# Norm sums turned one projection later, two projections issued ahead, and the rotary additions on GpSimd, in a two-layer hybrid encoder

## The chip, the cores and the metric

The kernel runs on one core of a Trainium2 chip. The metric is the device time of one execution in microseconds (us), lower is better; the time before is the median of three runs.

## The reference, cut to what matters

Two layers work on 512 tokens of width 1024. In each, one projection of the normalised input feeds three token mixers, which are gated, merged and projected out; a conv-gated MLP follows.

```python
h = RMSNorm(x); proj = h @ w_in          # one wide projection, split into
#  A: neighbourhood attention, 4 heads of 64, q and k RMS-normed per head
#  B: sliding-window attention, 8 q heads, 2 k/v heads, q/k normed, rotary on both
#  C: gated DeltaNet, 4 heads, chunks of 64 tokens, RMS-normed and gated output
#  merge gates: 3 x 1024 sigmoid gates
def apply_rope(x, cos, sin):
    x1, x2 = xf[..., :half], xf[..., half:]
    return jnp.concatenate([x1 * c - x2 * s, x2 * c + x1 * s], axis=-1)
```

The change touches the per-head norms of A's and B's queries and keys, and the rotation in B.

## The kernel before, in words

**Layout.** Activations lie as features on partitions and tokens along the free axis, in tiles of 128 x 512. A dense product is cut into chunks of 128 output features; `dense(l, c, rs)` makes one chunk. Weights and inputs are split in a high and a low part, and each of a chunk's 8 k-tiles takes three matmuls of 128 x 512 (`mm3`, L152 to L154: high by high, low by high, high by low), so a chunk is 24 matmuls. Its weights come in two halves of 4 k-tiles (256 KB each): SyncE's queue starts the transfer, ScalarE rounds the high part `wh` (L142), VectorE subtracts to get the low part `wl` (L144); for the chunks of the MLP GpSimd does that. Three buffers each hold raw, high and low halves.

**The projections of B** (`swa_project`): one chunk of keys (CH_SK), one of values (CH_SV), four of queries (CH_SQ to CH_SQ+3). **Of A** (`na_project`): twice a chunk of queries, keys and values (CH_NA+3j to CH_NA+3j+2). The first chunk of C's keys is CH_GK.

**A norm** squares the projection on ScalarE (`sq`) and calls `sums`: four small matmuls (L187) add the squares of each head into `pb`; ScalarE copies them to `sb` (L80); a TensorE transposition (L191) puts tokens on partitions. VectorE then computes the inverse root in nine short operations (`rsq`, L173 to L180). `spread` writes the factors into a 128 x 512 tile `rb` on VectorE (L201), four TensorE transpositions (L205) bring them back to the features' layout, and for a key L304 multiplies. Queries keep their factors by token, so only keys (`knorm`) and the output of C (`gdn_out`) use `spread`.

**The rotation** (`rope`, five times a layer: one key and four query tiles): a transfer by SyncE's queue makes `sw` with halves exchanged, GpSimd multiplies by the cosine (L310, `raw<-raw,fix`), VectorE multiplies `sw` by the sine (L311), and VectorE adds both (L312, `raw<-raw,sw`). Then ScalarE, VectorE and GpSimd split the result into `kdh`/`kdl` or `qs` (L476, L477, L504, L505).

**Order.** The stages are written in the order `sp np gg na gp sa gx gz gs gm gc go mn ms mg` (B's projections, A's projections, C's gates, A's attention, C's projections, B's attention, C's recurrence, its output `go`, the merges). Within that a scheduler of the framework picks the order of instructions on each engine when the kernel is built, and buffer pools limit it. `behind(m)` pins what stands in it to come after instruction `m` on its engine; `lastm[0]` is the last dense matmul written so far; `made` holds a chunk that was issued before its place. Dense chunks without a dependency (gates of the merges, for instance) are what the scheduler puts between small dependent steps.

**C's end** (`gdn_out`, twice a layer, j = 0 and 1): 32 small matmuls (L904, L908, tile `gd`), the square (L910), `sums`, L914, `rsq`, `spread`, and the gate (L916). Lines move in the changed kernel: L187 becomes L191, L191 becomes L198, L201 becomes L209, L205 becomes L213, L904 and L908 become L918 and L922, L310 to L312 become L322 to L324, L322 becomes L334, L477 becomes L489, L496 becomes L510.

Of the kernel before, what the change touches and what calls it, by code (L numbers as in the profile page):

```python
# [12 lines left out]
ALU = mybir.AluOpType  # L13
# [48 lines left out]
def encoder_kernel(ctx, tc, xT, wall, par, cst, nab, out, depth=2, dbg=None):  # L62
# [82 lines left out]
            ws += [(hi[:, k], lo[:, k]) for k in range(n)]  # L145
        return ws

    lastm, made = [None], {}

    def mm3(acc, w, r, start, stop):  # L150
        (wh, wl), (rh, rl) = w, r
# [1 line left out]
        T.matmul(acc, lhsT=wh, rhs=rl, start=False, stop=False)  # L153
        lastm[0] = T.matmul(acc, lhsT=wl, rhs=rh, start=False, stop=stop)  # L154

    def dense(l, c, rs):
        if (l, c) in made:
            return made.pop((l, c))
        ws = load_w(l, c)
        acc = bank("mm")  # L160
        for k, r in enumerate(rs):
            mm3(acc, ws[k], r, k == 0, k == len(rs) - 1)
        return acc

    def split(src, hi, lo):
# [16 lines left out]


    def sums(src, sel, tag, pb=None):
        pb = bank(tag)[:, 0:256] if pb is None else pb
        for b in range(4):
            T.matmul(pb[32 * b:32 * b + 32, 0:128], lhsT=sel, rhs=src[:, 128 * b:128 * b + 128], start=True, stop=True,  # L187
                     tile_position=(0, 32 * b))
        sb = tmp(shape=(128, 128), name="sb")
        copy("sb", sb, pb[:, 0:128])  # L190
        T.transpose(pb[:, 128:256], sb, ident)  # L191
        return pb[:, 128:256].rearrange("p (b i) -> p b i", b=4)[:, :, 0:32:16]


    def behind(m):
# [90 lines left out]
    for l in range(depth):  # L286
# [7 lines left out]
        y, mg, ma = {}, [], [None] * 8  # L294


        def knorm(raw, gain, dst, m=None):
            sq = tmp(name="sq")
            S.activation(out=sq, in_=raw, func=AF.Square)
            pb = sums(sq, halves, "at")  # L300
            a = small(8, "ka")
            V.tensor_scalar(a.rearrange("p (b e) -> p b e", e=2), pb, HD * EPS, None, op0=ALU.add)
            pr = spread(rsq(a, 8).rearrange("p (b e) -> p b e", e=2), 8.0, "at", m)
            V.scalar_tensor_tensor(dst, raw, gain, pr, op0=ALU.mult, op1=ALU.mult)  # L304

        def rope(qn):
            sw = tmp(name="sw")
            for b in range(4):
                nc.sync.dma_start(out=sw[32 * b:32 * b + 32], in_=qn[32 * (b ^ 1):32 * (b ^ 1) + 32])
            on("cos", "G").tensor_tensor(qn, qn, cosT, op=ALU.mult)  # L310
            on("sin", "V").tensor_tensor(sw, sw, sinT, op=ALU.mult)  # L311
            on("ropa", "V").tensor_tensor(qn, qn, sw, op=ALU.add)  # L312
            return qn

        def perm(a):
# [41 lines left out]
        def na_project():  # L357
            line[0] = "n"
            nonlocal naqk, vt, vt4, rns, irn

            xa = tmp(name="xa")
            S.activation(out=cr(xa), in_=perm(strm.acc), func=AF.Copy)
            naqk = []
            vt = [tmp(shape=(128, 4, 128), name="nvt") for _ in range(2)]
            vt4 = tmp(shape=(128, 4, 128), name="nvt4")
            pb = sums(xa, one, "at")
            an = small(16, "an")
            anv = an.rearrange("p (b f) -> p b f", f=4)
            mp = small(4, "mp")
            V.tensor_scalar(mp, pb[:, :, 0], HD * EPS / D, HD * EPS * EPS, op0=ALU.mult, op1=ALU.add)  # L370
            for j in range(2):
                qn, kn = tmp(name="qn"), tmp(name="kn")
                vn = tmp(name="nav")
                acc = dense(l, CH_NA + 3 * j, h)
                S.activation(out=cr(qn), in_=perm(acc), func=AF.Copy, scale=P[:, P_QK:P_QK + 1])
                sq = tmp(name="sq")
                S.activation(out=cr(sq), in_=perm(acc), func=AF.Square)
                pb = sums(sq, halves, "at")
                V.tensor_tensor(anv[:, :, 2 * j:2 * j + 2], mp.unsqueeze(2).to_broadcast([128, 4, 2]),
                                pb, op=ALU.add)  # L380
                kraw = permuted(dense(l, CH_NA + 3 * j + 1, h), tmp(name="raw"))
                permuted(dense(l, CH_NA + 3 * j + 2, h), vn)
                if j:
                    made[l, CH_GK] = dense(l, CH_GK, h)
                knorm(kraw, P[:, P_QK + 1:P_QK + 2], kn, lastm[0])
                qp, kh, kl = pair(F32R, name="nqs"), pair(F32R, name="nkh"), pair(F32R, name="nkl")
                naqk.append((qp, kh, kl))
                for e in range(2):
                    r = slice(64 * e, 64 * e + 64)
                    o = slice(64 - 64 * e, 128 - 64 * e)  # L390
                    S.activation(out=qp[e][r], in_=qn[r], func=AF.Copy)
                    on("nql", "G").tensor_tensor(qp[e][o], qn[r], qp[e].bitcast(F32)[r], op=ALU.subtract)
                    copy("nkh", kh[e][r], kn[r], "V")
                    S.activation(out=kh[e][o], in_=kn[r], func=AF.Copy)

                    on("nkl", "V").tensor_tensor(kl[e][r], kn[r], kh[e].bitcast(F32)[r], op=ALU.subtract)
                    G.memset(kl[e].bitcast(F32)[o], 0.0)
                pt = bank("at")
                for b in range(4):
                    k0, kn0 = (0, 64) if b == 0 else (128 * b - 64, 128)  # L400
                    T.transpose(pt[0:kn0, 128 * b:128 * b + 128], vn[:, k0:k0 + kn0], ident)
                S.activation(out=vt[j][0:64, 0], in_=pt[0:64, 0:128], func=AF.Copy)
                S.activation(out=vt[j][:, 1:4], in_=pt[:, 128:512].rearrange("p (b m) -> p b m", b=3), func=AF.Copy)
                pt = bank("at")
                T.transpose(pt[0:64, 0:128], vn[:, 448:512], ident)
                S.activation(out=vt4[0:64, j], in_=pt[0:64, 0:128], func=AF.Copy)
            rn = rsq(an, 16)
            rns = kept("rns", 16)
            V.tensor_scalar(rns, rn, -RSQ, None, op0=ALU.mult)
            irn = kept("irn", 16)  # L410
            V.scalar_tensor_tensor(irn, an, -1.0, rns, op0=ALU.mult, op1=ALU.mult)
# [53 lines left out]
        def swa_project():  # L465
            line[0] = "a"
            nonlocal kdh, kdl, vst, qs, rqs
            kr = scaled(dense(l, CH_SK, h), tmp(name="raw"))
            knorm(kr, P[:, P_QK + 3:P_QK + 4], kr)
            kr = rope(kr)  # L470
            kdh, kdl = pair(F32R, name="kdh"), pair(F32R, name="kdl")
            for gq in range(2):
                r = slice(64 * gq, 64 * gq + 64)
                o = slice(64 - 64 * gq, 128 - 64 * gq)
                copy("kdh", kdh[gq][r], kr[r], "V")
                S.activation(out=kdh[gq][o], in_=kr[r], func=AF.Copy)  # L476
                V.tensor_tensor(kdl[gq][r], kr[r], kdh[gq].bitcast(F32)[r], op=ALU.subtract)  # L477
                G.memset(kdl[gq].bitcast(F32)[o], 0.0)
            vf = scaled(dense(l, CH_SV, h), tmp(name="vf"))
            vst = tmp(name="sv")  # L480
            pt = bank("at")
            for b in range(4):
                T.transpose(pt[:, 128 * b:128 * b + 128], vf[:, 128 * b:128 * b + 128], ident)
            S.activation(out=vst, in_=pt, func=AF.Copy)

            qs = []
            aq = kept("aq")
            aqv = aq.rearrange("p (b f) -> p b f", f=8)
            for j in range(4):  # L489
                acc = dense(l, CH_SQ + j, h)  # L490
                qr = tmp(name="raw")
                S.activation(out=qr, in_=acc, func=AF.Copy, scale=P[:, P_QK + 2:P_QK + 3])
                sq = tmp(name="sq")
                S.activation(out=sq, in_=acc, func=AF.Square)
                pb = sums(sq, halves, "at")
                V.scalar_tensor_tensor(aqv[:, :, 2 * j:2 * j + 2], ms.unsqueeze(2).to_broadcast([128, 4, 2]), HD * EPS / D,  # L496
                                       pb, op0=ALU.mult, op1=ALU.add)
                qr = rope(qr)
                qp = pair(F32R, name="qs")
                for e in range(2):  # L500
                    r = slice(64 * e, 64 * e + 64)
                    o = slice(64 - 64 * e, 128 - 64 * e)
                    t = qp[e]
                    S.activation(out=t[r], in_=qr[r], func=AF.Copy)  # L504
                    on("ql", "G").tensor_tensor(t[o], qr[r], t.bitcast(F32)[r], op=ALU.subtract)  # L505
                qs.append(qp)
            rq = rsq(aq, 32)
            rqs = kept("rqs")
            V.tensor_scalar(rqs, rq, -RSQ, None, op0=ALU.mult)
# [664 lines left out]
```

## Time and profile before

| | |
|---|---|
| median of 3 runs | 1661.05 us (1659.44 to 1661.3) |
| the profiled execution, its own time | 1657.82 us |
| its span on the core | 1656.0 us |
| granted TensorE clock, mean | 0.998 |
| TensorE busy (matmuls) | 1626.6 us |
| VectorE busy | 1009.8 us |
| ScalarE busy | 767.0 us |
| GpSimd busy | 530.1 us |

The span is what the profiler saw from the first to the last instruction; 1.8 us of the execution lie outside it. A busy time is the sum over an engine's instructions. In the rows below PE is TensorE, DVE is VectorE, ACT is ScalarE, POOL is GpSimd; `out<-in` names the tiles with their buffer numbers left out, and an arrow in brackets names who ended a wait.

### The profile page before, as it was taken

How to read it: one execution, taken by the hardware profiler on the slowest of the kernel's cores; microseconds unless marked ns; L12 is line 12 of the kernel's file. 1: busy time of each engine (PE TensorE's matmuls, PEld its weight loads, DVE VectorE, ACT ScalarE, POOL GpSimd, SP SyncE). 2: the span in 40 equal slices, each digit the busy share in tenths (PEclk: the TensorE clock that was granted, in tenths of full speed). 3: DMA queues.
4: the chain of work that ended last, by engine and by line, in shares of the span. 5: the costliest groups of instructions: out<-in, count | busy, mean ns of one | idle time of the engine just before them, and what ended most of it. 6: DMA issues, size and time to landing. Idle time of an engine off the chain costs nothing.

```text
span 1656.0 us, 25095 instructions
## 1 busy us (share of the span) xinstructions
PE 1626.6 (98%) x9196; PEld 1300.2 (79%) x9196; DVE 1009.8 (61%) x1907; ACT 767.0 (46%) x1500; POOL 530.1 (32%) x512
## 2 busy tenths in 40 slices
PE   7999999998999999999999999999999999999999
PEld 5777787676888888878887777876788888888887
DVE  5699895454747777741137998855566577777200
ACT  5556666522444444443335665664234444444321
POOL 0333210130035554554406231102200455455543
PEclk9999999999999999999999999999999999999999
DMA  6222221121532323244333222111225322223442
GB/s 211 87 80 74 86 74 37 33 93 54 184 122 90 99 93 100 95 128 137 125 107 103 80 69 77 52 39 40 89 88 180 115 95 95 99 95 110 134 134 73
DMA packets 91499, 160.45 MB, mean 97 GB/s; under 512 B 10352, under 2 KB 17136, under 8 KB 91376
## 3 DMA queue, kind: packets, MB, share of 16 engines
q1 hardware_dynamic: 91376, 158.85, 29.7%
q8 instruction: 72, 1.18, 0.3%
q14 instruction: 51, 0.42, 0.1%
HBM read 147.80 MB, written 8.39 MB: 94 GB/s over the span
## 4 chain that ended last, share of the span: by engine, by line
PE 85%; DVE 5%; issue 4%; POOL 3%; ACT 2%; DMA 1%; SPq 0%; POOLq 0%; DVEq 0%; ACTq 0%
PE mm L152 24%; PE mm L154 24%; PE mm L153 24%; POOL wl L144 2%; PE at L560 1%; PE at L553 1%; DVE wl L144 1%; PE gd L710 1%; PE at L529 1%; PE at L456 1%; PE gd L843 1%; PE at L530 1%; PE gd L875 1%; PE gd L825 1%; PE gd L346 0%
## 5 line engine op out<-in xcount | busy, mean ns | idle before, releaser
L152 PE MATMUL mm<-hh,wh 128*128 128x512 f32 x1408 | 557.5, 396 | 11.2 <-ACT wh L142 9.9
L154 PE MATMUL mm<-hh,wl 128*128 128x512 f32 x1408 | 555.9, 395 | 5.2 <-DVE wl L144 5.1
L153 PE MATMUL mm<-hl,wh 128*128 128x512 f32 x1408 | 554.9, 395 | 0.5 <-DVE hl L222 0.5
L144 POOL TENSOR_TENSOR wl<-wr,wh 128x512 fp32r<-128x512 f32 (+1 forms) x272 | 363.3, 1347 | 556.7 <-ACT wh L142 545.3
L142 ACT ACTIVATE wh<-wr 128x512 fp32r<-128x512 f32 (+1 forms) x512 | 312.5, 617 | 328.1 <-PE mm L153 222.1
L152 PEld LDWEIGHTS mm<-hh,wh 128*128 128x128 f32 x1408 | 265.9, 189 | 71.5 <-ACT wh L142 12.4
L154 PEld LDWEIGHTS mm<-hh,wl 128*128 128x128 f32 x1408 | 265.9, 189 | 66.0 <-DVE wl L144 9.2
L153 PEld LDWEIGHTS mm<-hl,wh 128*128 128x128 f32 x1408 | 265.8, 189 | 59.0 <-DVE hl L222 3.0
L144 DVE TENSOR_TENSOR wl<-wr,wh 128x512 fp32r<-128x512 f32 x240 | 174.8, 731 | 97.9 <-ACT wh L142 93.5
L245 DVE SCALAR_TENSOR_TENSOR cv<-up,fix,cv 128x511 f32<-128x511 f32 x88 | 143.1, 1626 | 2.8
L154 PE MATMUL mm<-act,wl 128*128 128x512 f32 x352 | 137.1, 390 | 0.6 <-POOL wl L144 0.6
L244 DVE SCALAR_TENSOR_TENSOR cv<-up,fix,cv 128x511 f32<-128x511 f32 x88 | 83.0, 945 | 89.7 <-ACT cv L243 89.7
L152 PE MATMUL mm<-act,wh 128*128 128x512 f32 x352 | 137.1, 389 | 0.3 <-ACT wh L142 0.3
L153 PE MATMUL mm<-act,wh 128*128 128x512 f32 x352 | 137.0, 389 | 0.0
L243 ACT ACTIVATE cv<-up,fix 128x512 f32<-128x512 f32 x88 | 70.8, 809 | 35.5 <-DVE up L291 35.5
L166 ACT ACTIVATE act<-cv 128x512 fp32r<-128x512 f32 x44 | 27.8, 632 | 126.9 <-DVE cv L995 126.9
L154 PEld LDWEIGHTS mm<-act,wl 128*128 128x128 f32 x352 | 66.1, 188 | 15.3 <-POOL wl L144 1.2
L152 PEld LDWEIGHTS mm<-act,wh 128*128 128x128 f32 x352 | 66.1, 188 | 14.2 <-ACT wh L142 0.7
L153 PEld LDWEIGHTS mm<-act,wh 128*128 128x128 f32 x352 | 66.1, 188 | 13.7
L872 POOL TENSOR_TENSOR sd<-SA,fix 64x256 f32<-64x256 f32 x24 | 15.5, 646 | 177.5 <-DVE SA L882 135.5
L1013 DVE TENSOR_TENSOR xo<-xo,mm 128x512 f32<-128x512 f32 x8 | 5.5, 688 | 105.1 <-PE mm L154 105.1
L994 ACT ACTIVATE cv<-cv 128x512 f32<-128x512 f32 x44 | 27.8, 632 | 83.8 <-DVE cv L245 83.8
(292 smaller groups left out, 2153.1 us busy)
## 6 DMA issues: line engine op xcount, KB each, us to landing
wr<-in_wall_dram SPq DMA_DIRECT2D x496, 256.0 KB, 2.8
xs<-xo SPq DMA_DIRECT2D x16, 256.0 KB, 2.2
xo<-xs SPq DMA_DIRECT2D x16, 256.0 KB, 3.9
sw<-raw SPq DMA_DIRECT2D x40, 64.0 KB, 2.0
xf<-in_xT_dram SPq DMA_DIRECT2D x8, 256.0 KB, 6.2
xo<-in_xT_dram SPq DMA_DIRECT2D x8, 256.0 KB, 3.4
xf<-xs SPq DMA_DIRECT2D x8, 256.0 KB, 3.8
wr<-in_wall_dram SPq DMA_DIRECT2D x16, 128.0 KB, 3.1
```

The costliest lines, as they stand in the source:

```text
L142: S.activation(out=hi[:, :n], in_=raw[:, :n], func=AF.Copy)
L144: (G if c >= CH_UP else V).tensor_tensor(lo[:, :n], raw[:, :n], hi.bitcast(F32)[:, :n], op=ALU.subtract)
L152: T.matmul(acc, lhsT=wh, rhs=rh, start=start, stop=False)
L153: T.matmul(acc, lhsT=wh, rhs=rl, start=False, stop=False)
L154: lastm[0] = T.matmul(acc, lhsT=wl, rhs=rh, start=False, stop=stop)
L166: S.activation(out=hi, in_=src, func=AF.Copy)
L243: S.activation(out=dst, in_=src, func=AF.Identity, scale=w[:, 1:2], bias=bias)
L244: V.scalar_tensor_tensor(dst[:, 1:L], src[:, 0:L - 1], w[:, 0:1], dst[:, 1:L], op0=ALU.mult, op1=ALU.add)
L245: V.scalar_tensor_tensor(dst[:, 0:L - 1], src[:, 1:L], w[:, 2:3], dst[:, 0:L - 1], op0=ALU.mult, op1=ALU.add)
L456: T.matmul(py[64 * e:64 * e + 64, 128 * b_:128 * b_ + 128], lhsT=(vt[j][0:wi, b_ + i] if b_ + i < 4 else vt4[0:wi, j])[:, 64 * e:64 * e + 64],
L529: T.matmul(sc[:, 0:w], lhsT=q_, rhs=kdh[gq][:, kc], start=True, stop=False)
L994: S.activation(out=cv[0], in_=cv[0], func=AF.Silu)
```

## The change

The transposition of the norm sums is cut off from `sums` (`sums_from` returns `by_token(m)`), and is pinned behind the dense chunk that follows. For B's queries that chunk is issued ahead (`made`). `knorm` gets `first` (the values' projection, done between its sums and their transposition) and `then` (a chunk that is issued ahead; the transpositions of the factors are pinned behind it). So the value projection of B moves ahead of the key's rotation. And the rotation's addition moves from VectorE to GpSimd. `sums` is now `sums_from` with its transposition at once. The argument `m` of `dense` is not used.

```diff
+    def sums_from(src, sel, tag, pb=None):
         pb = bank(tag)[:, 0:256] if pb is None else pb
         ...
         copy("sb", sb, pb[:, 0:128])
-        T.transpose(pb[:, 128:256], sb, ident)
-        return pb[:, 128:256].rearrange("p (b i) -> p b i", b=4)[:, :, 0:32:16]
+        def by_token(m):
+            with behind(m):
+                lastt[0] = T.transpose(pb[:, 128:256], sb, ident)
+            return pb[:, 128:256].rearrange("p (b i) -> p b i", b=4)[:, :, 0:32:16]
+        return by_token
...
-        def knorm(raw, gain, dst, m=None):
+        def knorm(raw, gain, dst, first, then):
             sq = tmp(name="sq")
             S.activation(out=sq, in_=raw, func=AF.Square)
-            pb = sums(sq, halves, "at")
+            by_token = sums_from(sq, halves, "at")
+            first()
+            pb = by_token(lastm[0])
+            made[l, then] = dense(l, then, h)
+            m = lastm[0]
...
-            on("ropa", "V").tensor_tensor(qn, qn, sw, op=ALU.add)
+            on("ropa", "G").tensor_tensor(qn, qn, sw, op=ALU.add)
...
-                pb = sums(sq, halves, "at")
+                by_token = sums_from(sq, halves, "at")
+                kraw = permuted(dense(l, CH_NA + 3 * j + 1, h), tmp(name="raw"))
+                pb = by_token(lastm[0])
...
-                kraw = permuted(dense(l, CH_NA + 3 * j + 1, h), tmp(name="raw"))
-                permuted(dense(l, CH_NA + 3 * j + 2, h), vn)
-                if j:
-                    made[l, CH_GK] = dense(l, CH_GK, h)
-                knorm(kraw, P[:, P_QK + 1:P_QK + 2], kn, lastm[0])
+                knorm(kraw, P[:, P_QK + 1:P_QK + 2], kn, lambda: permuted(dense(l, CH_NA + 3 * j + 2, h), vn),
+                      CH_GK if j else CH_NA + 3)
...
-            knorm(kr, P[:, P_QK + 3:P_QK + 4], kr)
+            vf = tmp(name="vf")
+            knorm(kr, P[:, P_QK + 3:P_QK + 4], kr, lambda: scaled(dense(l, CH_SV, h), vf), CH_SQ)
...
-            vf = scaled(dense(l, CH_SV, h), tmp(name="vf"))
...
-                pb = sums(sq, halves, "at")
+                by_token = sums_from(sq, halves, "at")
+                nxt = CH_SQ + j + 1 if j < 3 else CH_NA
+                made[l, nxt] = dense(l, nxt, h)
+                pb = by_token(lastm[0])
```

The scheduler places everything else anew. On TensorE the matmuls are the same in both kernels; their order differs only within two stretches, one in each layer, from B's projections to the end of C.

**VectorE, layer 0, behind B's first query projection.** `kdh` and `kdl` are the key's split after its rotation, `nav` is A's value projection scaled, L311 or L323 the sine, L496 or L510 a query's sums. Before:

```order
L496 SCALAR_TENSOR_TENSOR fix<-fix,at 128x4x2
L312 TENSOR_TENSOR raw<-raw,sw 128x512
L496 SCALAR_TENSOR_TENSOR fix<-fix,at 128x4x2
L81 CAST kdh<-raw 64x512
L81 CAST kdh<-raw 64x512
L322 TENSOR_TENSOR nav<-mm,rstd 128x512
L311 TENSOR_TENSOR sw<-sw,fix 128x512
L477 TENSOR_TENSOR kdl<-raw,kdh 64x512
L477 TENSOR_TENSOR kdl<-raw,kdh 64x512
L144 TENSOR_TENSOR wl<-wr,wh 128x512
L312 TENSOR_TENSOR raw<-raw,sw 128x512
```

Of the change:

```order
L510 SCALAR_TENSOR_TENSOR fix<-fix,at 128x4x2
L334 TENSOR_TENSOR nav<-mm,rstd 128x512
L323 TENSOR_TENSOR sw<-sw,fix 128x512
L81 CAST kdh<-raw 64x512
L81 CAST kdh<-raw 64x512
L144 TENSOR_TENSOR wl<-wr,wh 128x512
L489 TENSOR_TENSOR kdl<-raw,kdh 64x512
L489 TENSOR_TENSOR kdl<-raw,kdh 64x512
L144 TENSOR_TENSOR wl<-wr,wh 128x512
```

Both additions are gone, and the weights' `wl` stands ahead of the key's `kdl` instead of behind it.

**TensorE, layer 0, the end of C's first half** (tile `gd_3111` is its sums, `gd_3130` its factors; `mm` are dense chunks of the merge gates). Before, after the last L908 of this half there are 22 dense matmuls, the sums (L187), 21 more dense matmuls, and then:

```order
L153 MATMUL mm_4243<-hl_151,wh_4239 128x512
L191 MATMUL gd_3111<-fix,sb_3116 128x128
L154 MATMUL mm_4243<-hh_150,wl_4241 128x512
L152 MATMUL mm_4243<-hh_159,wh_4239 128x512
L153 MATMUL mm_4243<-hl_160,wh_4239 128x512
L154 MATMUL mm_4243<-hh_159,wl_4241 128x512
L205 MATMUL gd_3130<-fix,rb_3128 128x128 x4
```

Of the change:

```order
L918 MATMUL gd_3074<-qd_474_2138,SA_2898 64x64
L918 MATMUL gd_3074<-qd_475_2139,SA_2898 64x64
L922 MATMUL gd_3074<-Q_2125,VN_2782 64x64 x2
L191 MATMUL gd_3111<-sq_3108,fix 32x128 x4
L198 MATMUL gd_3111<-fix,sb_3116 128x128
L213 MATMUL gd_3130<-fix,rb_3128 128x128 x4
L918 MATMUL gd_3140<-qd_476_2140,SA_2895 64x64
```

No dense matmul is left from the half's last L922 to its factors' transpositions; those chunks now stand ahead, between the steps of C's recurrence. On VectorE nothing stands within that chain (L928 to L209) any more; before, L291 (`gt`) and one L144 did.

**TensorE, layer 1, the same place.** Before, 21 dense matmuls lie between the sums and L191 and 37 between L191 and L205, which ends so:

```order
L154 MATMUL mm_11989<-hh_7447,wl_11981 128x512
L152 MATMUL mm_11989<-hh_7561,wh_11985 128x512
L153 MATMUL mm_11989<-hl_7562,wh_11985 128x512
L205 MATMUL gd_10876<-fix,rb_10874 128x128 x4
L904 MATMUL gd_10886<-qd_2078_9886,SA_10641 64x64
```

Of the change, again with 21 dense matmuls between the sums and the first row's transposition:

```order
L198 MATMUL gd_10857<-fix,sb_10862 128x128
L154 MATMUL mm_11989<-hh_7789,wl_11987 128x512
L152 MATMUL mm_11989<-hh_7903,wh_11985 128x512
L153 MATMUL mm_11989<-hl_7904,wh_11985 128x512
L154 MATMUL mm_11989<-hh_7903,wl_11987 128x512
L213 MATMUL gd_10876<-fix,rb_10874 128x128 x4
L918 MATMUL gd_10886<-qd_2078_9886,SA_10641 64x64
```

Four dense matmuls are left between the two, and in VectorE's row one `gt` and one `wl` still stand within the chain.

## Rows read from the trace of the kernel before

**Rows 1.** The page: busy time of the engines, and the chain that ended last.

```profile
PE 1626.6 (98%) x9196; PEld 1300.2 (79%) x9196; DVE 1009.8 (61%) x1907; ACT 767.0 (46%) x1500; POOL 530.1 (32%) x512
PE 85%; DVE 5%; issue 4%; POOL 3%; ACT 2%; DMA 1%; SPq 0%; POOLq 0%; DVEq 0%; ACTq 0%
```

**Rows 2.** TensorE's waits, 60 to 160 us: us in total, times, longest.

```profile
PE mm L154 <- DVE wl L144: 1.8, 2, 1.3
PE mm L152 <- DVE kn L304: 1.1, 1, 1.1
PE at L205 <- DVE rb L201: 0.8, 1, 0.8
PE at L187 <- DVE abd L586: 0.7, 1, 0.7
```

**Rows 3.** TensorE's waits, 860 to 960 us.

```profile
PE mm L154 <- DVE wl L144: 1.7, 1, 1.7
PE mm L152 <- ACT wh L142: 1.5, 1, 1.5
PE at L191 <- ACT sb L80: 1.1, 1, 1.1
```

**Rows 4.** TensorE's waits, 260 to 430 us: recurrence and end of C, layer 0.

```profile
PE gd L205 <- DVE rb L201: 2.6, 1, 2.6
...
PE gd L875 <- DVE VN L866: 0.6, 1, 0.6
...
PE gd L863 <- DVE SA L880: 0.3, 1, 0.3
```

**Rows 5.** VectorE's row around 75 us: start, duration.

```profile
72.98 0.69 DVE L144 TENSOR_TENSOR wl<-wr,wh 128x512 fp32r<-128x512 f32 x1
...
77.10 1.77 DVE L144 TENSOR_TENSOR wl<-wr,wh 128x512 fp32r<-128x512 f32 x1
```

**Rows 6.** GpSimd's row in the same stretch.

```profile
69.79 1.29 POOL L310 TENSOR_TENSOR raw<-raw,fix 128x512 f32<-128x512 f32 x1 [1.53 <-DMA sw<-raw]
75.08 4.94 POOL L505 TENSOR_TENSOR qs<-raw,qs 64x512 fp32r<-64x512 f32 x3 [4.00 <-ACT qs L504]
```

**Rows 7.** Line L312, the additions: duration in ns (least, median, most), idle before.

```profile
L312 DVE TENSOR_TENSOR raw<-raw,sw x10: 679/692/1780, 66.4 to 903.5; 128x512 f32<-128x512 f32 x10
...
  POOL raw L310: 4.9, 3
```

**Rows 8.** TensorE, end of C's first half, layer 0: start, duration.

```profile
374.40 0.29 PE L908 MATMUL gd<-Q,VN 128*64 128x64 f32 x4
...
379.83 0.46 PE L187 MATMUL gd<-sq,fix 128*32 128x128 f32 x8
...
385.16 0.27 PE L191 MATMUL gd<-fix,sb 128*128 128x128 f32 x1
...
388.95 0.66 PE L205 MATMUL gd<-fix,rb 128*128 128x128 f32 x4 [2.61 <-DVE rb L201]
```

**Rows 9.** ScalarE in the same place.

```profile
374.79 0.60 ACT L910 ACTIVATE sq<-gd 128x512 f32<-128x512 f32 x1 [0.84 <-PE gd L908]
...
380.53 0.26 ACT L80 ACTIVATE sb<-gd 128x128 f32<-128x128 f32 x1
```

**Rows 10.** VectorE in the same place.

```profile
385.46 0.17 DVE L914 TENSOR_TENSOR fix<-gd,fix 128x8 f32<-128x8 f32 x1 [0.74 <-PE gd L191]
...
386.39 0.69 DVE L291 TENSOR_TENSOR gt<-mm,rstd 128x512 f32<-128x512 f32 x1
...
387.07 0.68 DVE L144 TENSOR_TENSOR wl<-wr,wh 128x512 fp32r<-128x512 f32 x1
...
388.47 0.43 DVE L201 TENSOR_SCALAR rb<-fix 128x512 f32<-128x512 f32 x1
```

**Rows 11.** TensorE, the same place in layer 1.

```profile
1200.01 0.27 PE L191 MATMUL gd<-fix,sb 128*128 128x128 f32 x1
...
1208.53 0.60 PE L205 MATMUL gd<-fix,rb 128*128 128x128 f32 x4
```

More of the change, by code (lines that the diff above doesn't have):

```diff
@@ L146, in load_w @@
         return ws
-    lastm, made = [None], {}
+    lastm, lastt, made = [None], [None], {}
     def mm3(acc, w, r, start, stop):
@@ L154, in mm3, with dense @@
         lastm[0] = T.matmul(acc, lhsT=wl, rhs=rh, start=False, stop=stop)
-    def dense(l, c, rs):
+    def dense(l, c, rs, m=None):
         if (l, c) in made:
@@ L160, in dense @@
         acc = bank("mm")
-        for k, r in enumerate(rs):
-            mm3(acc, ws[k], r, k == 0, k == len(rs) - 1)
+        with behind(m):
+            for k, r in enumerate(rs):
+                mm3(acc, ws[k], r, k == 0, k == len(rs) - 1)
         return acc
@@ L184, in sums @@
     def sums(src, sel, tag, pb=None):
+        return sums_from(src, sel, tag, pb)(None)
+    def sums_from(src, sel, tag, pb=None):
         pb = bank(tag)[:, 0:256] if pb is None else pb
@@ L190, in sums @@
         copy("sb", sb, pb[:, 0:128])
-        T.transpose(pb[:, 128:256], sb, ident)
-        return pb[:, 128:256].rearrange("p (b i) -> p b i", b=4)[:, :, 0:32:16]
+        def by_token(m):
+            with behind(m):
+                lastt[0] = T.transpose(pb[:, 128:256], sb, ident)
+            return pb[:, 128:256].rearrange("p (b i) -> p b i", b=4)[:, :, 0:32:16]
+        return by_token
     def behind(m):
```

## The prediction

> **What bounds the kernel now.** I read the page first: TensorE is busy 98% of the span and holds 85% of the chain that ended last [rows 1]. So the time is the sum of TensorE's work and its waits, and the built order has the same matmuls in both kernels; a matmul that only changes its place costs nothing. What can change is where TensorE stands still. The list of its waits over the two stretches in which the order differs says how much there is to win: 4.4 us in four kinds of place in layer 0's projections [rows 2], 4.3 us in layer 1's [rows 3], and in the recurrence and end of C one wait of 2.6 us and small ones of 0.9 us together [rows 4]. The largest gain that this change can make is thus 8.7 us from the projections and 3.5 us behind them, 0.7% of 1661.
>
> Only one of all these waits is for the copy of norm sums (L191 for `sb`, 1.1 us), which the pinning is made to hide, and two more are for a key's norm (L205 for `rb`, 0.8, and a dense matmul behind `kn`, 1.1). The largest are for `wl` on VectorE and `wh` on ScalarE: the weights come late, because the engine that prepares them is held by other work.
>
> **The change, part by part.**
>
> *The additions.* Ten leave VectorE, with a median of 0.69 us and 1.78 at most [rows 7]. Half of them lie at the median or under it and the others at up to 1.78, so between 6.9 and 5 x 0.69 + 5 x 1.78 = 12.4 us of busy time go; I take 10. With them go the 4.9 us in which VectorE stood still for GpSimd's cosine. On GpSimd an addition has the shape of the cosine's product, 1.29 us [rows 6]; ten are 13 us on an engine that is busy 32% of the span. A key or query is ready later by some 0.6 us each (1.29 for 0.69), and the splits behind it wait so long; they are read only in B's attention, far behind.
>
> *What a GpSimd operation does to VectorE.* The same subtraction `wl` took 0.69 us at 72.98, with GpSimd idle, and 1.77 us at 77.10, within GpSimd's 4.94 us of L505 [rows 5, 6]. So each GpSimd operation that overlaps a VectorE operation on two tiles can hold it for about 1.08 us. Ten additions on GpSimd could hand back at most 10 x 1.08 = 10.8 us, all of the 10; at least nothing. I take half, since the additions fall partly on short norm operations and on those with one operand in PSUM. The Trainium skill ("SBUF — State Buffer", section "Who interferes with whom") has a rule for it: a VectorE instruction with two SBUF inputs and a GpSimd instruction that reads SBUF need one shared read interface, and whoever starts first keeps it for the whole instruction. These two rows agree; by the rule each addition of 1.29 us on GpSimd could block VectorE for its full length, and the sum would be that of the rival on the other side.
>
> *The projections.* In layer 0 the longer of the two `wl` waits (1.3 us) is for the one that stands behind `kdh`, `nav`, the sine and `kdl` on VectorE; in the new row an addition is gone before it and both `kdl` stand behind it. That is worth more than the 1.3 us, if GpSimd's addition for the key is done when `kdh` wants it; I give it half. The other `wl` wait (0.5) depends on GpSimd's operations, and I leave it. The waits for `rb` and `kn` (1.9) are answered by the pinning: the factors' transpositions stand behind one more chunk of 24 matmuls. In the built order the second key's factors now lie much earlier on VectorE relative to the convolutions of C. I take these as gone, and the 0.7 as left. Layer 0: 0.6 + 1.9 = 2.5. In layer 1 the wait for `sb` (1.1) goes, since a whole chunk stands ahead of that transposition, and the 1.7 for `wl`, behind a norm's short operations and an addition, goes too with the addition and the new order; of the 1.5 for `wh` I take half, as ScalarE's queries move but not its load. Layer 1: 1.1 + 1.7 + 0.7 = 3.5. Against these 6.0 us I set 1.3 for new waits of the same kind, one typical wait from the two lists, since every weight half still has to pass VectorE in a new order. Net gain 4.7; bounds 0 and 8.7.
>
> *The recurrence.* More dense matmuls stand between its steps (24 each from the middle on). Its waits of 0.6 and 0.3 in layer 0 [rows 4] go: 0.9.
>
> *The end of C.* Here the order takes away what hid a chain. In layer 0 the chain now runs bare from the half's last L908 to its factors. From rows: L908 begins at 374.40, ScalarE's square ends at 374.79 + 0.60 = 375.39 [rows 8, 9], 0.99 us. From the sums' start to the end of `sb`: 379.83 to 380.79, 0.96 us. From L191 to L205: 385.16 to 388.95, 3.79 us [rows 8], in which VectorE's chain from L914 to L201 holds `gt` and `wl`, 0.69 and 0.68 [rows 10]; they are gone in the new row, and 2.4 us stay. The sum is 4.4 us, of which about 0.6 us are TensorE's own small matmuls, which cost that before too (an estimate: between half and all of the 0.29, 0.46 and 0.27 of [rows 8], since matmuls overlap). So some 3.8 us of wait, for 2.6 before [rows 4]: +1.2. In layer 1 there were 37 dense matmuls between L191 and L205 (8.52 us in all, 0.23 each) and no wait [rows 11]; now there are four, with `gt` and `wl` within the chain. That is the picture of layer 0 before (four dense matmuls, both operations in the chain), where the wait was 2.6: +2.6. Second halves: 10 dense matmuls (2.3 us) stay between the two transpositions in layer 0, for a chain of 2.4, about nothing. End of C: +3.8, with bounds of 2.8 (ScalarE and VectorE answer sooner) and 6 (a weight half or a gate gets in between in both layers).
>
> *Sum.* -4.7 - 0.9 + 3.8 = -1.8. The profiled execution took 1657.8 us (1656.0 of span and 1.8 outside it) and becomes 1656.0; it lay 3.2 us below the median of the runs, so against the median the forecast is 1661.05 - 1.8 = 1659.3 us. A measurement of this kernel tells about 0.2% (3.3 us) from no change; this is within it.
>
> **The rivals.**
>
> *The projections run clean.* All 8.7 us and the 0.9 go, and the end of C costs 2.8: -6.8, 1654.2 us. For it: every wait in those two lists but one names VectorE or a norm, and VectorE loses 10 us of work and 4.9 of waiting. Against it: part of these waits is ScalarE's, and GpSimd takes back some.
>
> *GpSimd holds VectorE (the other side).* Each addition on GpSimd holds a `wl` by 1.08 us where weights are short; VectorE gains nothing, the 8.7 us stay in other places, and the end of C costs 4 to 6: +4.5, 1665.5 us. It decides from the point at which about 8 of the 10 additions hold a VectorE operation. For it: the two rows of 0.69 and 1.77, and the additions themselves, stretched from 0.69 to up to 1.78. Against it: GpSimd did stand idle for 4.00 us before L505 [rows 6], so the key's addition finds room.
>
> *The change does next to nothing.* The pins agree with what the scheduler did anyway, and the end of C finds cover from instructions that arrive at other times than planned: 1661 us, within 1 us.
>
> **How the numbers follow.** Forecast case (gain in the projections given back at C's end, 1656.5 to 1662.5): 0.45. Projections clean: 0.27. GpSimd holds VectorE: 0.15. Next to nothing: 0.13. Faster by over 0.2% means below 1657.7: the second case and a fifth of the first, 0.36. Slower means above 1664.4: the third case and a little of the first, 0.16. Within 0.2%: 0.48. The range reaches from 1653.5, just beyond the clean case, to 1665.5, the held case.
>
> **What would show it.** In the changed trace: TensorE's waits between 60 and 160 us and between 860 and 960 us should add up to about 4 us instead of 8.7, with L198 waiting for nothing; L213 for `rb` at C's end should wait 3.8 us in layer 0 and 2.6 us in layer 1; the recurrence should have no wait for SA or VN in layer 0; GpSimd's L324 should take 1.3 to 1.8 us, and some `wl` next to it 1.77 instead of 0.69. I am wrong if the waits at C's end are under 1 us (another dense matmul arrives there), or if the projections' waits exceed 8 us.

## The result: 1671.85 us, slower by 0.77%

The changed kernel takes 1671.85 us (median of four runs, 1670.16 to 1673.54) against 1660.24 us of the kernel before, measured beside it: a ratio of 1.0077, 95% interval 1.0065 to 1.0089. It lies outside the range that was given, on the side of the rival "GpSimd holds VectorE", and 6 us beyond even that.

The page of the changed kernel, busy times and the granted clock in 40 slices:

```profile
PE 1637.8 (98%) x9196; PEld 1310.4 (78%) x9196; DVE 1016.7 (61%) x1897; ACT 766.5 (46%) x1500; POOL 543.3 (33%) x522
...
PEclk9989999999999999999999999999999999999999
```

Two things stand out against [rows 1]. TensorE runs the same 9196 matmuls and is busy 11.2 us longer: its clock must have been lower for a while. And VectorE lost ten additions, yet is busy 6.9 us longer, so other operations of it have become longer. The span grew by 15.8 us: 11.2 of TensorE's busy time and 4.6 of standing still. (The two profiled executions lie 2.4 us under and 1.7 us over the medians, so some 4 of the 15.8 us are spread between executions; the medians differ by 11.6.)

TensorE's waits in the changed kernel, first 60 to 160 us:

```profile
PE mm L152 <- DVE fix L181: 2.8, 1, 2.8
PE mm L154 <- DVE wl L144: 1.5, 2, 1.1
PE at L213 <- DVE rb L209: 1.1, 1, 1.1
PE at L198 <- ACT sb L80: 0.7, 1, 0.7
```

860 to 1000 us:

```profile
PE mm L154 <- DVE wl L144: 5.2, 2, 3.1
```

360 to 440 us, the end of C in layer 0:

```profile
PE gd L213 <- DVE rb L209: 2.4, 1, 2.4
PE gd L191 <- ACT sq L924: 0.8, 1, 0.8
PE gd L198 <- ACT sb L80: 0.4, 1, 0.4
```

1190 to 1245 us, the end of C in layer 1:

```profile
PE gd L213 <- DVE rb L209: 2.6, 1, 2.6
```

The end of C came as worked out: 2.4 + 0.8 + 0.4 = 3.6 us in layer 0 (3.8 forecast) and 2.6 in layer 1 (2.6 forecast). The projections did not: 6.1 us in layer 0 and 5.2 in layer 1, where [rows 2, 3] had 4.4 and 4.3 and 4 in all was forecast. The largest in layer 0 is new, a dense matmul at 99 us that waits 2.8 us:

```profile
99.05 0.47 PE L152 MATMUL mm<-hh,wh 128*128 128x512 f32 x1 [2.78 <-DVE fix L181]
```

What VectorE did there, start and duration:

```profile
89.98 1.08 DVE L174 TENSOR_SCALAR fix<-fix 128x32 int32<-128x32 int32 x1
91.10 1.23 DVE L175 SCALAR_TENSOR_TENSOR fix<-fix 128x32 f32<-128x32 f32 x1
92.36 1.34 DVE L176 SCALAR_TENSOR_TENSOR fix<-fix 128x32 f32<-128x32 f32 x1
...
96.44 1.30 DVE L179 SCALAR_TENSOR_TENSOR fix<-fix 128x32 f32<-128x32 f32 x1
...
97.77 0.19 DVE L180 SCALAR_TENSOR_TENSOR fix<-fix 128x32 f32<-128x32 f32 x1
97.88 1.02 DVE L334 TENSOR_TENSOR nav<-mm,rstd 128x512 f32<-128x512 f32 x1
```

And GpSimd at the same time:

```profile
89.28 2.99 POOL L324 TENSOR_TENSOR raw<-raw,sw 128x512 f32<-128x512 f32 x2
92.35 5.33 POOL L519 TENSOR_TENSOR qs<-raw,qs 64x512 fp32r<-64x512 f32 x4
```

This is the inverse root of the queries' norms, 32 columns, a chain of eight short steps (L174 to L181). A step takes 0.19 us when GpSimd no longer reads (97.77, beside GpSimd's writing of zeros) and 1.23 to 1.34 us beside GpSimd's additions and splits, which is the length of one GpSimd operation (5.33 / 4 = 1.33). Nearly each step waits for one. Behind the chain in VectorE's queue stands `nav` (97.88 to 98.90), which empties a PSUM bank of the dense chunks, and the matmul starts at 99.05. (The list names L181, the step that ended last before it, which is no operand of a dense matmul.) In the kernel before, `nav` stood ahead of the root, and of the root's steps in this layer only the first was held:

```profile
92.39 1.07 DVE L322 TENSOR_TENSOR nav<-mm,rstd 128x512 f32<-128x512 f32 x1
...
95.16 1.08 DVE L173 TENSOR_SCALAR fix<-fix 128x32 int32<-128x32 int32 x1
96.27 0.19 DVE L174 SCALAR_TENSOR_TENSOR fix<-fix 128x32 f32<-128x32 f32 x1
```

In layer 1 the longest wait, 3.1 us, lies behind the same root, there interleaved with a key's: it runs from 922.22 to 929.64, and the awaited `wl` comes next in VectorE's queue (the matmul starts at 930.29).

```profile
929.56 0.68 DVE L144 TENSOR_TENSOR wl<-wr,wh 128x512 fp32r<-128x512 f32 x1
```

The granted clock in five stretches of the changed kernel (columns: length, then busy time of PE, PEld, DVE, ACT and POOL, the granted clock, DMA share, GB/s):

```profile
100.00:114.00 14.00, 12.87 (x58) 10.16 (x58) 11.16 (x29) 6.38 (x16) 0.00 (x0) 0.52 0.14 43
...
403.00:408.00 5.00, 4.99 (x72) 4.48 (x73) 2.07 (x3) 1.23 (x2) 0.00 (x0) 0.66 0.01 3
906.00:910.00 4.00, 3.99 (x13) 2.91 (x17) 2.53 (x3) 1.31 (x3) 1.28 (x1) 0.57 0.45 131
930.00:937.00 7.00, 6.71 (x33) 4.91 (x34) 5.98 (x11) 2.39 (x7) 0.60 (x2) 0.51 0.35 112
1226.00:1231.00 5.00, 5.00 (x73) 4.40 (x71) 2.48 (x4) 1.75 (x3) 0.00 (x0) 0.66 0.09 31
```

Each stretch follows a place where TensorE stood still: the 2.8 and 1.1 us around 100 us, the 3.6 us before 403, waits of 2.1 and 3.1 us that ended at 906 and 930, the 2.6 us before 1226. In them the clock is at or falls to half (1.2 of 2.4 GHz). What each lost of full clock is its length by what is missing to 1.00: 6.7, 1.7, 1.7, 3.4 and 1.7 us, 15.2 us, about as much as the waits ahead of them (3.9, 3.6, 2.1, 3.1 and 2.6: 15.3 us). A sixth stretch, 250 to 258 us at 0.57 (3.4 us lost), has its like in the kernel before.

### The profile page after: what moved, and what is told of

Its sections match the earlier page's. It is cut to its first block, busy times and chain, and to the rows that moved or that the text cites. A ratio compares the mean times of both kernels' runs of the same rounds, so it can differ in the third digit from the quotient of the medians.

```text
span 1671.8 us, 25091 instructions
## 1 busy us (share of the span) xinstructions
PE 1637.8 (98%) x9196; PEld 1310.4 (78%) x9196; DVE 1016.7 (61%) x1897; ACT 766.5 (46%) x1500; POOL 543.3 (33%) x522
## 4 chain that ended last, share of the span: by engine, by line
PE 89%; DVE 4%; issue 3%; POOL 2%; DMA 1%; ACT 1%; SPq 0%; POOLq 0%; DVEq 0%; ACTq 0%
PE mm L152 25%; PE mm L154 25%; PE mm L153 25%; POOL wl L144 2%; PE at L574 1%; PE at L567 1%; DVE wl L144 1%; PE gd L724 1%; PE at L543 1%; PE gd L857 1%; PE gd L889 1%; PE at L467 1%; PE gd L877 1%; PE gd L839 1%; PE at L544 1%
## 5 line engine op out<-in xcount | busy, mean ns | idle before, releaser
L144 POOL TENSOR_TENSOR wl<-wr,wh 128x512 fp32r<-128x512 f32 (+1 forms) x272 | 363.0, 1345 | 563.6 <-ACT wh L142 547.5
L144 DVE TENSOR_TENSOR wl<-wr,wh 128x512 fp32r<-128x512 f32 x240 | 176.5, 738 | 95.4 <-ACT wh L142 92.2
L154 PEld LDWEIGHTS mm<-act,wl 128*128 128x128 f32 x352 | 66.1, 188 | 15.3 <-POOL wl L144 1.5
```

The costliest lines, as they stand in the source:

```text
L144: (G if c >= CH_UP else V).tensor_tensor(lo[:, :n], raw[:, :n], hi.bitcast(F32)[:, :n], op=ALU.subtract)
```

## The experiments

Each kernel is built anew, and the scheduler then places everything again. So one compares two orders as well as two edits, and a chain's own rows say more than a total. Each ratio is to the kernel before, measured beside the run.

**The order alone.** The changed kernel with the addition back on VectorE.

```diff
-            on("ropa", "G").tensor_tensor(qn, qn, sw, op=ALU.add)
+            on("ropa", "V").tensor_tensor(qn, qn, sw, op=ALU.add)
```

> The change with the rotation's additions back on VectorE, so the pinned sums and the chunks issued ahead alone. Theory A (GpSimd holds VectorE: its additions push the queries' splits under the short norm operations, 1.3 us each instead of 0.19): the wait of 2.8 us at 96 us and the two of 2.1 and 3.1 us in layer 1's projections go, TensorE's waits in the projections add up to under 6 us, half clock after them is gone; the waits at the end of C (3.6 and 2.6 us) stay as far as that order stays; 1660 to 1664 us. Theory B (the order of the pinned work itself makes VectorE late): the long waits stay, 1669 to 1673 us.

1660.6 us against 1658.46: ratio 1.0009, 1.0 to 1.0019. Its page:

```profile
PE 1626.5 (98%) x9196; PEld 1302.3 (79%) x9196; DVE 1012.5 (61%) x1907; ACT 767.4 (46%) x1500; POOL 528.2 (32%) x512
```

TensorE's busy time is back at that of before. The waits in the projections are nearly those of [rows 2, 3] (1.9 for `wl`, 0.9 for `rb`, 0.7 for `abd` in layer 0; 1.8, 1.3 and 1.1 in layer 1), and the end of C waits 2.6 us and 2.5 us. So the pins cost about what they save, and the wait for `sb` that they were meant to end is still there: 1.1 us.

**The additions alone.** The kernel before with that one line changed the other way.

> The kernel before with only the rotation's additions moved to GpSimd; no pins. Theory A: waits of 2 us and more for wl or behind a held norm appear in the projections, with a half clock after them, 1666 to 1672 us. Theory B: no loss from the additions, 1656 to 1661 us.

1671.03 us: ratio 1.0073, 1.0056 to 1.009. Waits from 60 to 160 us:

```profile
PE mm L152 <- DVE fix L180: 2.8, 1, 2.8
```

and VectorE there:

```profile
91.36 1.23 DVE L174 SCALAR_TENSOR_TENSOR fix<-fix 128x32 f32<-128x32 f32 x1
92.62 1.34 DVE L175 SCALAR_TENSOR_TENSOR fix<-fix 128x32 f32<-128x32 f32 x1
```

The same wait, the same stretched steps, `nav` behind them again, half clock at the same places, TensorE busy 1637.6 us: one line makes the loss. It also empties the end of C in both layers, with no pin in the kernel: waits of 3.6 us in layer 0 (2.4, 0.8 and 0.4) and 3.3 us in layer 1.

**Half of the order each.** Additions on VectorE; first only the queries' pins, then only the keys'.

```diff
# queries only: knorm as in the kernel before
-            by_token = sums_from(sq, halves, "at")
-            first()
-            pb = by_token(lastm[0])
-            made[l, then] = dense(l, then, h)
+            pb = sums(sq, halves, "at")
```

> Of the change only the queries' part: their sums turned behind the next projection, that projection issued ahead; keys as before, additions on VectorE. Under A within 3 us of the kernel before, 1658 to 1663 us. Under B, if the queries' pins are what delays VectorE, 1666 to 1672 us.

1658.4 us, ratio 0.9999 (0.999 to 1.0009).

```diff
# keys only: the queries' sums as in the kernel before
-                by_token = sums_from(sq, halves, "at")
-                nxt = CH_SQ + j + 1 if j < 3 else CH_NA
-                made[l, nxt] = dense(l, nxt, h)
-                pb = by_token(lastm[0])
+                pb = sums(sq, halves, "at")
```

> Of the change only the keys' part: value projection ahead, one more chunk ahead of the factors' transpositions; queries as before, additions on VectorE. Under A within 3 us of the kernel before, 1658 to 1663 us. Under B, if the keys' part is what moves the chunks out of the end of C and delays VectorE, 1666 to 1672 us.

1659.96 us, ratio 1.0014 (1.0005 to 1.0023). The queries' pins show no effect: the waits of layer 0's projections are those of [rows 2] to a tenth. The keys' part brings the second wait at the end of C (2.5 us in layer 1), and a little loss.

**The hold, taken away from the root.** The changed kernel, with the running value `y` of the queries' root in PSUM. Its steps then read one SBUF tile and one in PSUM; only the squaring (L177) still reads an SBUF tile twice. GpSimd's work is the same.

```diff
-    def rsq(a, n):
-        y, t = small(n, "rq"), small(n, "rt", 1)
+    def rsq(a, n, y=None):
+        y, t = small(n, "rq") if y is None else y, small(n, "rt", 1)
...
-            rq = rsq(aq, 32)
+            rq = rsq(aq, 32, bank("at")[:, 0:32])
```

> The changed kernel, with one thing altered: the running value of the queries' inverse root (32 columns) lies in PSUM, so that of its short VectorE operations only two read two SBUF tiles. Theory A1 (an operation with two SBUF operands is held for as long as a GpSimd operation runs): the steps that took 1.23 to 1.34 us beside GpSimd's splits fall to about 0.2 us, except the one that squares an SBUF tile, so the chain of 9 us shrinks by some 5 us, the wait of 2.8 us at 96 us and half of the 15 us of half clock after it go; 1662 to 1667 us. Theory A2 (VectorE is merely slow beside GpSimd, whatever it reads): the steps stay at 1.3 us and the time at 1670 to 1674 us.

1657.11 us: ratio 0.9991, 0.9981 to 1.0. VectorE (`at` is the PSUM tile):

```profile
91.23 0.20 DVE L174 TENSOR_SCALAR at<-fix 128x32 int32<-128x32 int32 x1
...
91.90 0.42 DVE L177 SCALAR_TENSOR_TENSOR fix<-fix 128x32 f32<-128x32 f32 x1
92.36 0.20 DVE L178 SCALAR_TENSOR_TENSOR at<-fix,at 128x32 f32<-128x32 f32 x1
92.58 0.19 DVE L179 SCALAR_TENSOR_TENSOR fix<-at,fix 128x32 f32<-128x32 f32 x1
...
93.03 0.20 DVE L181 SCALAR_TENSOR_TENSOR at<-fix,at 128x32 f32<-128x32 f32 x1
```

with GpSimd beside it:

```profile
88.83 3.44 POOL L324 TENSOR_TENSOR raw<-raw,sw 128x512 f32<-128x512 f32 x2
92.35 6.03 POOL L519 TENSOR_TENSOR qs<-raw,qs 64x512 fp32r<-64x512 f32 x4
```

GpSimd runs its additions and its splits through the whole chain, and the steps take 0.2 us but for the squaring, 0.42: 2.0 us for the chain (91.23 to 93.23) instead of 9.0 (89.98 to 99.00). The clock stays full where it was at half:

```profile
100.00:114.00 14.00, 13.71 (x86) 11.15 (x85) 12.61 (x42) 9.17 (x23) 0.88 (x2) 1.00 0.18 58
```

That decides between the two forms of the theory: it is what a step reads that holds it (for the first step, which reads one tile in both kernels, where it writes), not that GpSimd runs. The total lies 14.7 us under the change, more than the 5 to 10 expected; part of that is the new order, in which `nav` stands ahead of the root again (89.42) and the end of C in layer 0 has no wait any more. How the 14.7 us divide between the hold and the order was not measured.

**The splits moved from beside the root.** The changed kernel, GpSimd's splits of the last two queries queued behind the root. To pin them there, the scaling of the root's result moves to GpSimd too, one operation of 128 x 32 a layer.

```diff
-                    on("ql", "G").tensor_tensor(t[o], qr[r], t.bitcast(F32)[r], op=ALU.subtract)
+                    if j >= 2:
+                        later.append((t[o], qr[r], t.bitcast(F32)[r]))
...
-            V.tensor_scalar(rqs, rq, -RSQ, None, op0=ALU.mult)
+            with behind(G.tensor_scalar(rqs, rq, -RSQ, None, op0=ALU.mult)):
+                for lo, q_, hi_ in later:
+                    on("ql", "G").tensor_tensor(lo, q_, hi_, op=ALU.subtract)
```

> The changed kernel, with GpSimd's splits of the last two queries queued behind the queries' inverse root instead of beside it; the additions stay on GpSimd. Theory A1: the root's steps take 0.2 us except those beside an addition, the wait at 96 us falls under 1 us and the half clock after it goes, 1662 to 1667 us. If the loss comes from the additions' own time and not from what they push under the root: no change, 1669 to 1673 us.

1662.15 us: ratio 1.002, 1.0011 to 1.0029. VectorE, a step of the queries' root and two of the next key's:

```profile
92.93 0.20 DVE L176 SCALAR_TENSOR_TENSOR fix<-fix 128x32 f32<-128x32 f32 x1
...
96.14 1.20 DVE L176 SCALAR_TENSOR_TENSOR fix<-fix 128x8 f32<-128x8 f32 x1
...
97.58 1.14 DVE L178 SCALAR_TENSOR_TENSOR fix<-fix 128x8 f32<-128x8 f32 x1
```

The queries' root runs free from its third step on (the first two, beside the additions, still take 1.08 and 1.24 us), and the splits now hold the root of the key that follows, where TensorE waits 4.1 us for `rb`. The hold moves with GpSimd's work; half clock there is some 7 us long instead of 14.

**Matmuls in place of the wait.** The changed kernel with 36 useless matmuls in layer 0, behind the chunk that ends at 94 us.

```diff
             made[l, then] = dense(l, then, h)
             m = lastm[0]
+            if l == 0 and then == CH_GK:
+                dm = bank("gd")
+                for k in range(36):
+                    with behind(m):
+                        m = T.matmul(dm, lhsT=h[k % 8][0][:, 0:128], rhs=h[k % 8][0], start=k == 0, stop=k == 35)
```

> The changed kernel plus 36 useless matmuls of 128 x 512 (8.2 us at full clock) on TensorE in layer 0, behind the chunk that ends at 94 us, so that they fill the waits of 2.8 and 1.1 us there. Theory C (the waits are dear because the clock falls to half behind them): the clock stays at 1.00 from 94 to 115 us, the 14 us of half clock there (7 us lost) go, and 8.2 us of added work are paid by 3.9 us of waits and 7 us of clock: 1668 to 1672 us, not slower than the change. Without the clock (waits alone matter): 8.2 less 3.9 us slower, 1675 to 1678 us.

1670.24 us: ratio 1.0068, 1.0054 to 1.0082, not told apart from the change (1.0077). Only 16 of the 36 came to stand ahead of the wait, and it was not filled:

```profile
94.41 3.79 PE L317 MATMUL gd<-hh 128*128 128x512 f32 x16
102.58 1.07 PE L213 MATMUL at<-fix,rb 128*128 128x128 f32 x4 [4.38 <-DVE rb L209]
```

The clock fell behind it as well, for 4 us instead of 14; TensorE is busy 1633.4 us in all, 4.4 less than in the change's profile with 36 matmuls more. That speaks for the clock's part of the loss. But it was meant to keep the clock up and didn't, so it is no proof, and that the time lies in the range given for this case is luck.

**Fewer VectorE operations instead.** The kernel before, with the casts of the keys on ScalarE.

```diff
-ENG = {}
+ENG = {"kdh": "S", "nkh": "S"}
```

> The kernel before, with the key's and A's keys' casts (kdh, nkh: two of 64 x 512 each, 0.9 us apiece beside GpSimd) moved from VectorE to ScalarE, no pins and no additions moved. If it is GpSimd's hold on VectorE that makes weights late in the kernel before, then less VectorE work in those stretches with no more on GpSimd shortens the waits of 4.4 and 4.3 us by 2 to 4 us: 1654 to 1658 us. If ScalarE's own queue then makes wh late: 1658 to 1663 us.

1652.45 us: ratio 0.9961, 0.9949 to 0.9974. Faster than both kernels, and than the 1654 to 1658 expected. Its waits, 60 to 160 us:

```profile
PE at L205 <- DVE rb L201: 1.3, 2, 1.1
PE gd L589 <- DVE abd L586: 0.9, 1, 0.9
```

and 860 to 1000 us:

```profile
PE mm L154 <- DVE wl L144: 1.4, 1, 1.4
```

8.7 us of waits in the projections have become 3.6. In all twelve casts left VectorE: two for each of the six keys.

**What the cures are worth apart and together.** The kernel before with only the root in PSUM:

> The kernel before, with only the running value of the queries' inverse root in PSUM. Control for the run that did this to the changed kernel: if PSUM only took back what the additions had put under the root, little is to be had here, since of its steps only the first, of 1.08 us, was held: 1656 to 1660 us, a gain of 0 to 2 us. If PSUM is good for the order as such, 3 us and more.

1654.53 us: ratio 0.9973, 0.9962 to 0.9983. A gain of 5.0 us, more than the 0 to 2 that held steps were to explain; no wait for `kn`, `rb` or `abd` is left in layer 0's projections and 1.2 us in layer 1's. The expectation counted one held step. The trace of the kernel before has three: the first in layer 0 (1.08 us) and, in layer 1, the first and the third (1.08 and 1.17 us), some 2.8 us beyond their 0.19. How the gain divides between the hold and the new order is open. The whole change with both cures:

> The whole change with both cures: the queries' root with its running value in PSUM, and the casts kdh and nkh on ScalarE. If GpSimd's hold on operations with two SBUF operands is all that was wrong with the change, the additions on GpSimd are now worth what was hoped: 1648 to 1653 us, at or under the kernel before with the casts moved alone (1652.5). If the weights' low halves, which have two SBUF operands and can't be cured so, still meet GpSimd: 1653 to 1658 us.

1658.76 us: ratio 0.9999, 0.999 to 1.0008. A miss: 1648 to 1653 us was expected if the hold was all that was wrong, and 1653 to 1658 if not. Its waits in the projections are the smallest of all, 1.0 and 0.4 us; 3.3 us at the end of C in layer 1 and small waits in the recurrence remain, and TensorE is busy 1630.3 us, 4 us over [rows 1]. The order with the casts but without additions or PSUM:

> The pins and the chunks issued ahead without the additions, with the casts kdh and nkh on ScalarE. The casts gave the kernel before 6.6 us; if the order is neutral apart from the end of C (2.5 us worse in layer 1), 1653 to 1656 us; if pins and casts help each other, under 1651 us.

1653.36 us: ratio 0.9963, 0.9951 to 0.9976, the same as the casts alone. So the whole change with both cures is 0.36% slower than this (0.9999 against 0.9963). The two differ by the additions and by the root in PSUM, and which of them costs it is open; `kdl` is still held in the cured change (1.45 us each on average, 0.96 before). And the kernel before with the casts and both roots, queries' and keys', in PSUM:

> The kernel before with the casts on ScalarE and the running value of the roots of queries and keys in PSUM; additions on VectorE, no pins. If less VectorE work and fewer holds add up: 1648 to 1652 us. If the casts already took what was there: 1651 to 1654 us.

1665.03 us: ratio 1.0037, 1.0024 to 1.0051. A miss: the projections wait little, but A's attention and what follows has new waits (over the whole run):

```profile
PE at L445 <- DVE lg L442: 2.5, 1, 2.5
PE mm L152 <- ACT y L461: 2.4, 3, 1.2
PE gd L875 <- DVE VN L866: 2.3, 4, 1.0
```

with half clock around 190 and 215 us among other places. Why the scheduler's order came out so is open; PSUM banks kept longer by the keys' root are a guess that was not tried.

## Why the prediction was wrong

**The mechanism was named, as the rival; its price was wrong.** In the sum the term that failed is the projections: -4.7 us, with bounds of 0 and 8.7 for the gain, where their waits rose by 2.6 (8.7 to 11.3); only 1.3 us for new waits stood against the gain. The step behind it reads: "Ten additions on GpSimd could hand back at most 10 x 1.08 = 10.8 us, all of the 10; at least nothing. I take half, since the additions fall partly on short norm operations and on those with one operand in PSUM." PSUM does free an operation, as the run with the root there shows; the rest fails. A short operation is not cheap to hold: it waits for the GpSimd operation, not for a share of its own time, 0.19 us becoming 1.33. And it is not the additions alone that count. They fill GpSimd's idle time, and in layer 0 the root's first two steps run beside two additions (89.28 to 92.27) and the next four beside four splits (92.35 to 97.68), so that in a chain of dependent steps nearly each one meets a GpSimd operation. VectorE's busy time measures it: 1009.8 less some 10 for the additions (their rows add up to 11.0) should have been 1000; it is 1016.7, so some 17 us were handed back, not 5. About 9 of them are the roots' steps of 32 columns in the two layers. Another 5 are the key's split, its subtraction `kdl` (6.8 us for 3.8) and, with one SBUF operand only, its casts (busy time, mean length in ns, idle time before):

```profile
L81 DVE CAST kdh<-raw 64x512 fp32r<-64x512 f32 x4 | 4.7, 1187 | 0.1
```

Before:

```profile
L81 DVE CAST kdh<-raw 64x512 fp32r<-64x512 f32 x4 | 2.7, 664 | 0.1
```

The runs with the additions alone (1.0073) and the order alone (1.0009) show that the additions make the loss, and the run with the root in PSUM that what the root's steps read and write in SBUF is what holds them. The wait of 2.8 us also rests on `nav` standing behind the root, as it does in layer 0 of the change and of the additions alone, and not in the kernel before or with the order alone.

The Trainium skill has the rule ("SBUF — State Buffer", section "Who interferes with whom"), and more of it than the prediction used: an instruction of VectorE with at most one SBUF input, outside its two-port modes, does not contend. The trace agrees: 0.19 and 0.20 us beside GpSimd with one SBUF operand, 1.2 to 1.3 with two. The same section counts casts and tensor_scalar among the operations that can contend in a two-port mode. That agrees with the casts above, and with the root's first step, which has one SBUF input: 1.08 us into SBUF, 0.20 us into PSUM.

**A term was missing: the clock.** The sum priced a wait by its length and put what follows it at nothing. In the changed kernel TensorE's busy time grew by 11.2 us with the same matmuls, more than twice the 4.6 us by which it stood still longer: by size this is the larger failure. The rows of [rows 2 to 4] had no such tail; before, half clock shows in two short places, some 4 us at 247 and 1063 us each, some 3.4 us of full clock lost for 18.6 in the change's six stretches. The rival of 1665.5 us lacked the term too. That the waits bring the half clock is argued from their order in time; the one run that set out to keep the clock up did not manage it.

**The projections.** Forecast 4 us of waits, measured 11.3. The wait for the `wl` behind the key's split did shrink (0.45 us for 1.3), as its place in the order said, but another of 1.1 us appeared behind `kdl`, whose two operations grew from 1.40 to 3.47 us there; the wait for `sb` is gone in layer 1, and one of 0.7 us is new in layer 0. In layer 1 TensorE waits 5.2 us for `wl`: 2.1 behind `kdl` (3.37 us for two) and 3.1 behind the root, GpSimd's additions and splits being beside VectorE there as well.

**The end of C and the recurrence were right.** 3.6 and 2.6 us of bare chain against 3.8 and 2.6; no wait in the list from 260 to 360 us, as forecast. (The full list behind [rows 4] has four more small waits, 2.1 us together, which the sum left out; all but 0.2 us went too.) The half clock behind those two places was not in the sum. What emptied them was put down to the pins; the additions alone do it too.

**The additions' own time was right**: 1.28 to 1.74 us each on GpSimd, 14.1 us in all for the 13 forecast; GpSimd's busy time grew by 13.2 (530.1 to 543.3).

## What to carry to other kernels

Work that goes from VectorE to GpSimd can be paid by each VectorE operation with two SBUF operands that then runs beside it (here by casts from SBUF to SBUF as well), by up to the length of a GpSimd operation and however short it is itself. Look for chains of short dependent steps in the stretch, put one operand in PSUM or keep GpSimd idle there, and ask first whether ScalarE can take the work: here twelve casts on ScalarE gave 0.39%, where ten additions on GpSimd cost 0.73%. A cure need not make the move pay: with the root in PSUM the change was no faster (0.9991) than the kernel before with the root in PSUM (0.9973). And where TensorE is the bound, look at the granted clock behind a wait before pricing it by its length: here 15.3 us of waits were followed by 15.2 us of lost clock, and TensorE's busy time grew by 11.2.

## What the hardware showed that was not expected

Nearly the same wait is followed by half clock in one kernel and not in another. In the kernel before the 2.61 us at the end of C [rows 4, 8] are followed by full clock:

```profile
389.00:395.00 6.00, 6.00 (x83) 5.19 (x84) 2.13 (x3) 1.34 (x3) 0.00 (x0) 1.00 0.12 39
```

With the queries' pins alone a wait of 2.60 us in the same place, with the same dense matmuls ahead of it, is followed by half clock:

```profile
387.03 0.66 PE L213 MATMUL gd<-fix,rb 128*128 128x128 f32 x4 [2.60 <-DVE rb L209]
...
386.00:392.00 6.00, 4.97 (x72) 4.61 (x73) 2.25 (x6) 1.23 (x2) 0.00 (x0) 0.72 0.16 46
```

What tells them apart is not settled here. How long the half clock lasts differs as well: 4 us behind a wait of 2.1, 7 behind one of 3.1, and 14 where two waits and a run of small matmuls follow each other.
